# The last quarter of a feed-forward block: the norm carried by the rows, residual additions made by transfers, the last product in the banks of the one before it

## The chip, the cores and the metric

The kernel runs on one core of one Trainium2 chip. The metric is the device time of one execution in microseconds (us). A profile comes from one execution; its span runs from the first to the last instruction and is a little shorter than the time.

## What is computed

One layer of a streaming encoder over 512 frames (columns here) and 1024 channels, then a final norm. Everything is float32. Three branches (banded attention, a gated recurrence and latent attention) are gated, merged and projected, and the result is added to x. The part that matters here is what follows:

```
h2 = rmsnorm(x, norm_ffn_g)                    # x: 512 frames, 1024 channels
x  = x + square(relu(h2 @ w_ff1)) @ w_ff2      # 4096 hidden channels
return rmsnorm(x, final_norm_g)
```

The kernel keeps channels on the 128 partitions and frames in the free dimension, so x is eight tiles `x2[m]` of 128 channels x 512 frames, and a norm needs a sum over partitions, which TensorE makes with a matrix of ones.

## The kernel before, in words

Matrix products are exact to float32 by three matmuls each (`mm3`): every operand is split into a high and a low part, and high x high, high x low and low x high are summed. So each weight block of 128x1024 is cast on ScalarE (`wh`) and its rest taken on VectorE (`wl`) before TensorE can use it. There are two tiles for raw weights (`wr`) and three each for `wh` and `wl`.

The norm's factor rstd per frame is not applied before w_ff1: it is a positive factor per frame, so square(relu(.)) of the unnormed product is taken, and rs2 (rstd squared) is multiplied in behind w_ff2.

The hidden channels are treated in four quarters (`for q in range(4)`). For each, `first(q)` makes eight 128-channel blocks by w_ff1 (`gemm`, 24 matmuls of 512 frames each, tile `p`), squares them on ScalarE into a tile r (`rf`) and forms, for each of four row groups i, the seven operands that a Strassen-Winograd scheme needs: A11, A12, A22, S3, S1, S2, S4, each 128x256 with a high part (`rh`) and a low part (`rl`). "A" and "S" are sums and differences of the quadrants that two hidden halves and two halves of the frames make. Then seven half-size products with w_ff2 follow, 48 matmuls of 256 frames each:

| product | left operand (weights) | right operand | into banks | is taken into |
|---|---|---|---|---|
| 1 | b11 | A11 | `ba` (sa) | c11 |
| 2 | a sum of blocks | S1 | `bc` (sc) | m22 |
| 3 | b21 | A12 | `bb` (sb) | c11 |
| 4 | a sum | S2 | `ba`, on top | m12 |
| 5 | b22 | S4 | `bc`, on top | m12 |
| 6 | a sum | S3 | `ba`, on top | m22 |
| 7 | a sum | A22 | new `bb` (sb) | c21, with `ba` |

The sums of weight blocks are made by transfers: `chain` loads a block through SP's queue (tiles `cw` and `ew`) and adds further blocks to it by adding transfers that POOL issues. `take` copies a pair of banks to a pair of tiles in `out` (ScalarE), or adds it there (VectorE). The four results c11, m12, c21 and m22 (m12 and m22 with a minus sign) are the four quadrants of the residual: half of the frames (th) x half of the channels (ch).

Their sums over quarters 0 to 2 are multiplied by rs2 and added to x2 inside `first(3)` (`residual`, after each row group i). In quarter 3 (`last`) the tiles start afresh, and each quadrant is finished as soon as it is complete: `resid` multiplies by rs2 on VectorE (L1291) and adds to x2 on VectorE (L1294). `squares` squares each piece of x2 on ScalarE (L1314), adds the squares up (L1317) and scales the piece by the final gain on ScalarE, in place (L1318). The first two squares of each half of the frames go to the two parts of a tile `fin`; the other six to scratch tiles from `fw`, whose body is

```
temps.append(temps.pop(0))
return temps[-1]
```

with three tiles in `temps`. `finish_half(th)` sums the squares over the channels with three matmuls of ones (`pst`, L1325), makes 1/sqrt with `rstd_of` (L257, L242 to L251: three scratch tiles v, l and r0, all from `fw`; r0 is the result, rf), multiplies the eight pieces of that half by it (L1331, six on VectorE, two on POOL) and sends them out through SP's queue (L1332).

TensorE's instructions run in the order in which the code issues them (`manual_schedule`). In the other queues a planner sets the order, by the order of the code and by when it thinks that operands are ready; what stands in `urgent()` (weight loads, casts and the adding transfers of `chain`) goes first. Waits between engines are set by what an instruction reads and writes: a tile that is handed out again is not written before its last reader is done. In quarter 3 the code has `finish_half(0)` between products 6 and 7, and `finish_half(1)` at the end.

Of the kernel before, what the change touches and what calls it, by code (L numbers as in the profile page):

```python
# [9 lines left out]
F32 = mybir.dt.float32  # L10
F32R = mybir.dt.float32r
I32 = mybir.dt.int32
AF = mybir.ActivationFunctionType
# [4 lines left out]
S = 512  # L18
P = 128
# [121 lines left out]
def _body(ctx, tc, ap, dbgo):  # L141
# [112 lines left out]
    def rstd_of(new, psum, n, w=S, behind=None):  # L254

        v = new("st_v")[:, :w]
        V.tensor_scalar(v, psum, 1.0 / n, EPS, ALU.mult, ALU.add)  # L257
        return rsqrt(new, v, behind=behind)
# [897 lines left out]
    with ExitStack() as f_ctx:  # L1156
# [4 lines left out]
        def fw(n):  # L1161
            temps.append(temps.pop(0))
            return temps[-1]
# [34 lines left out]
        def pair(x):  # L1198
            return x.rearrange("p (a c) -> p a c", a=2)

        def first(q):

            ops = []
            for i in range(4):
                rh = fp.tile([P, 7, H], F32R, tag="rh", name="rh", bufs=4)
                rl = fp.tile([P, 7, H], F32R, tag="rl", name="rl", bufs=4)
                r = fp.tile([P, 8, H], F32, tag="rf", name="rf", bufs=1)
                a21 = r[:, 7]
                for j in range(2):
# [10 lines left out]
                A.copy(rh[:, 0:3], r[:, 0:3])  # L1220
# [3 lines left out]
                V.tensor_tensor(rl[:, 0:3], r[:, 0:3], f(rh[:, 0:3]), ALU.subtract)  # L1224
                A.copy(rh[:, 3:7], r[:, 3:7])
                V.tensor_tensor(rl[:, 3:7], r[:, 3:7], f(rh[:, 3:7]), ALU.subtract)
                ops.append((rh, rl))
                if q == 3:
                    residual(i)
            return ops  # L1230
# [38 lines left out]
                    start and i == 0 and t % 2 == 0, i == 3, skip_group_check=True)  # L1269


        where = dict(c11=(0, 0, ALU.add), m12=(0, 1, ALU.subtract), c21=(1, 0, ALU.add), m22=(1, 1, ALU.subtract))
        out = {}

        def take(name, banks):

            if name in out:
                for b in range(2):
                    V.tensor_tensor(out[name][b], out[name][b], banks[b], ALU.add)
            else:  # L1280
                out[name] = [act.tile([P, S], F32, tag="act", name=name) for _ in range(2)]
                for b in range(2):
                    A.copy(out[name][b], banks[b])

        def resid(name, b, src, ts=(0, 1)):

            th, ch, op = where[name]
            n = slice(th * H, th * H + H)
            u = out[name][b]
            k = slice(ts[0], ts[-1] + 1)  # L1290
            V.tensor_tensor(pair(u)[:, k], pair(src)[:, k], rs2[:, n].unsqueeze(1).to_broadcast([P, len(ts), H]), ALU.mult)  # L1291
            for t in ts:
                m = ch * 4 + 2 * b + t
                V.tensor_tensor(x2[m][:, n], x2[m][:, n], pair(u)[:, t], op)  # L1294

        def residual(i):

            name = ('c11', 'm12', 'c21', 'm22')[i]
            for b in range(2):
                resid(name, b, out[name][b])  # L1300

        sqs = {}

        def squares(name, b, ts=(0, 1)):
            th, ch, _ = where[name]
            n = slice(th * H, th * H + H)
            for t in ts:
                m = ch * 4 + 2 * b + t
                sq = sqs.setdefault(th, [])
                if len(sq) < 2:  # L1310
                    d = fin[th][:, len(sq)]
                else:
                    d = fw("sq")[:, :H]
                A.activation(d, x2[m][:, n], AF.Square)  # L1314
                sq.append(d)
                if 2 < len(sq) < NK:
                    V.tensor_tensor(sq[len(sq) % 2], sq[len(sq) % 2], d, ALU.add)  # L1317
                A.activation(x2[m][:, n], x2[m][:, n], AF.Copy, scale=g_fin[:, m:m + 1])  # L1318

        def finish_half(th):  # L1320
            n = slice(th * H, th * H + H)
            pst = ptp("pst")[:, :H]
            sq = sqs[th]
            for i, d in enumerate((sq[0], sq[1], sq[-1])):
                T.matmul(pst, ones, d, start=i == 0, stop=i == 2)  # L1325
            rf = rstd_of(fw, pst, D, w=H)
            for i in range(NK // 2):
                o = fp.tile([P, 2, H], F32, tag="xg", name="o", bufs=16)
                for j in range(2):
                    m = 2 * i + j  # L1330
                    (G if m in (2, 5) else V).tensor_tensor(o[:, j], x2[m][:, n], rf, ALU.mult)  # L1331
                nc.sync.dma_start(ap['out'][2 * i * P:2 * (i + 1) * P, n].rearrange("(a p) c -> p a c", p=P), o)  # L1332

        for q in range(4):
            last = q == 3
            (b11, b12), (b21, b22) = ([ap['w_ff2'][q, i, j] for j in range(2)] for i in range(2))
            ts = chain(b11, [b12, b22, b21], "cw", 1)
            t3 = chain(b22, [b12], "ew", 1)
            ops = first(q)
            if last:  # L1340
                out.clear()
                fin = [pair(fp.tile([P, S], F32, tag="xg", name="fin", bufs=16)) for _ in range(2)]
                left = [fp.tile([P, S], F32, tag="xg", name="left", bufs=16) for _ in range(2)]

            def plain(b):
                return [stream(b[i], eng=V) for i in range(2)]

            ba = [psc("sa") for _ in range(2)]
# [4 lines left out]
            take('m22', bc)  # L1353
# [7 lines left out]
            product(ba, ts(), ops, S2, False)  # L1361
            take('m12', ba)
            product(bc, plain(b22), ops, S4, False)
            take('m12', bc)
# [18 lines left out]
            if last:  # L1383
                for b in range(2):
                    for t in range(2):
                        resid('c21', b, bb[b], (t,))
                        squares('c21', b, (t,))
            else:
                take('c21', bb)
        finish_half(1)  # L1390

# [14 lines left out]
```

## Time and profile before

| | |
|---|---|
| median of 3 runs | 954.14 us (952.27 to 956.85) |
| the profiled execution | 951.3 us, span 949.5 us |
| granted TensorE clock, mean | 0.984 |
| busy: PE, DVE, ACT, POOL | 907.1, 657.1, 557.5, 201.4 us |
| quarter 3: `first(3)`, seven products, the rest | from 844.3, 887.9 and 930.4 us of the span |

PE is TensorE's matmuls, PEld its weight loads, DVE VectorE, ACT ScalarE, POOL GpSimd, SP the engine that issues most transfers. A row of the order of instructions gives start and duration in us, engine, line, operation, output <- inputs by the program's names, shapes, a count, and in brackets how long the engine had been idle before and who released it. A row of a group gives busy time and mean ns. A row on transfers gives their count, KB each, and the median us from issue to landing.

### The profile page before, as it was taken

To read this page: it belongs to the slowest core of one execution; us is meant where nothing else is said; L and a number is where in the kernel's file an instruction comes from. 1 tells how busy PE (TensorE), PEld (TensorE's weight loads), DVE (VectorE), ACT (ScalarE), POOL (GpSimd) and SP (SyncE) were. 2 spreads that over 40 slices of the span, in tenths; PEclk is the share of its full clock that TensorE was granted. 3 is DMA by queue.
4 is the path that set the end of the run, shared out by engine and by line. 5 is a ranking of instruction groups with operands and counts; after the bars stand their busy time and mean duration, and the time that the engine had idled before them with its cause. 6 is when DMAs were issued, how large, how long until landed. Compare 5 with 4: busy or idle time off the path is not lost.

```text
span 949.5 us, 13636 instructions
## 1 busy us (share of the span) xinstructions
PE 907.1 (96%) x5070; PEld 784.4 (83%) x5070; DVE 657.1 (69%) x1212; ACT 557.5 (59%) x983; POOL 201.4 (21%) x264
## 2 busy tenths in 40 slices
PE   8889999998998899999999999999999999999993
PEld 6578898987877788888888888889989988998992
DVE  6488888787878869788472454455456745885686
ACT  7556778787776656757552444555365346435663
POOL 4422101111154424333122122001101100110002
PEclk9899999999999999999999999999999999999996
DMA  6865445666666475758689784238835862893522
GB/s 200 212 132 120 91 93 115 140 123 125 139 128 144 97 157 111 155 115 195 137 203 207 165 236 140 89 92 196 227 108 133 209 190 89 182 240 111 132 47 89
DMA packets 42947, 138.08 MB, mean 145 GB/s; under 512 B 5056, under 2 KB 9296, under 8 KB 42880
## 3 DMA queue, kind: packets, MB, share of 16 engines
q0 software_dynamic: 23104, 83.95, 43.8%
q1 hardware_dynamic: 19776, 53.26, 16.8%
q8 instruction: 40, 0.66, 0.3%
q14 instruction: 27, 0.22, 0.1%
HBM read 135.03 MB, written 2.16 MB: 144 GB/s over the span
## 4 chain that ended last, share of the span: by engine, by line
PE 72%; DVE 15%; issue 4%; DMA 4%; ACT 3%; POOL 1%; SPq 0%; DVEq 0%; POOLq 0%; ACTq 0%
PE p L227 6%; PE p L228 6%; PE p L226 6%; PE pj L325 3%; PE pj L321 3%; PE pj L323 3%; PE pg L321 3%; PE pg L325 3%; PE pg L323 3%; PE sa L228 2%; PE sa L227 2%; PE sa L226 2%; PE sc L522 2%; DMA bias<-in_rel 2%; PE po L227 2%
## 5 line engine op out<-in xcount | busy, mean ns | idle before, releaser
L221 ACT CAST wh<-wr 128x1024 fp32r<-128x1024 f32 x64 | 67.2, 1050 | 111.0 <-PE p L227 24.8
L222 DVE TENSOR_TENSOR wl<-wr,wh 128x1024 fp32r<-128x1024 f32 x64 | 78.3, 1223 | 75.9 <-ACT wh L221 67.5
L226 PE MATMUL p<-x2h,wh 128*128 128x512 f32 x256 | 100.0, 391 | 0.0
L227 PE MATMUL p<-x2l,wh 128*128 128x512 f32 x256 | 99.6, 389 | 0.0
L228 PE MATMUL p<-x2h,wl 128*128 128x512 f32 x256 | 99.6, 389 | 0.0
L279 ACT ACTIVATE wl<-wh 128x1024 fp32r<-128x1024 f32 x64 | 67.7, 1057 | 48.4 <-PE pg L325 26.9
L321 PE MATMUL pg<-xgh,wh 128*128 128x512 f32 x192 | 76.7, 400 | 0.0
L325 PE MATMUL pg<-xgh,wl 128*128 128x512 f32 x192 | 76.6, 399 | 0.0
L323 PE MATMUL pg<-xgl,wh 128*128 128x512 f32 x192 | 76.3, 398 | 0.0
L321 PE MATMUL pj<-xgh,wh 128*128 128x512 f32 x160 | 65.0, 406 | 2.4 <-ACT c L429 2.4
L323 PE MATMUL pj<-xgl,wh 128*128 128x512 f32 x160 | 65.7, 410 | 0.0
L325 PE MATMUL pj<-xgh,wl 128*128 128x512 f32 x160 | 64.3, 402 | 0.8 <-DMA wl<-in_w_aqk 0.8
L1256 POOL DMA_DIRECT2D cw<-in_w_ff x16 | 13.7, 858 | 219.2 <-DVE wl L1236 216.4
L226 PEld LDWEIGHTS p<-x2h,wh 128*128 128x128 f32 x256 | 48.1, 188 | 10.1 <-issue 0.2
L227 PEld LDWEIGHTS p<-x2l,wh 128*128 128x128 f32 x256 | 48.1, 188 | 10.1 <-issue 0.2
L228 PEld LDWEIGHTS p<-x2h,wl 128*128 128x128 f32 x256 | 48.1, 188 | 10.0
L227 PE MATMUL sa<-rl,wh 128*128 128x256 f32 x192 | 54.3, 283 | 0.0
L228 PE MATMUL sa<-rh,wl 128*128 128x256 f32 x192 | 54.3, 283 | 0.0
L226 PE MATMUL sa<-rh,wh 128*128 128x256 f32 x192 | 54.3, 283 | 0.0
L1236 DVE TENSOR_TENSOR wl<-cw,wh 128x1024 fp32r<-128x1024 f32 x24 | 29.3, 1223 | 29.9 <-ACT wh L1235 29.9
L1235 ACT CAST wh<-cw 128x1024 fp32r<-128x1024 f32 x24 | 25.2, 1050 | 35.0 <-PE sc L227 11.1
L321 PEld LDWEIGHTS pg<-xgh,wh 128*128 128x128 f32 x192 | 36.9, 192 | 7.8 <-DVE tg L884 0.4
(406 smaller groups left out, 2807.7 us busy)
## 6 DMA issues: line engine op xcount, KB each, us to landing
wr<-in_w_ff SPq DMA_DIRECT2D x56, 512.0 KB, 3.5
wh<-in_w_g POOLq DMA_DIRECT2D x24, 512.0 KB, 3.9
wl<-in_w_g POOLq DMA_DIRECT2D x24, 512.0 KB, 6.1
cw<-in_w_ff POOLq DMA_DIRECT2D x24, 512.0 KB, 5.6
wh<-in_w_br POOLq DMA_DIRECT2D x12, 512.0 KB, 3.8
wl<-in_w_br POOLq DMA_DIRECT2D x12, 512.0 KB, 6.1
wh<-in_w_aqk POOLq DMA_DIRECT2D x8, 512.0 KB, 4.4
wl<-in_w_aqk POOLq DMA_DIRECT2D x8, 512.0 KB, 6.4
```

Source lines behind the costliest of these rows:

```text
L221: A.copy(hi[:, :n], r[:, :n])
L222: (eng or G).tensor_tensor(lo[:, :n], r[:, :n], f(hi[:, :n]), ALU.subtract)
L226: T.matmul(out, wh, xh, start=start, stop=False, **kw)
L227: T.matmul(out, wh, xl, start=False, stop=False, **kw)
L228: T.matmul(out, wl, xh, start=False, stop=stop, **kw)
L279: A.activation(lo, f(hi), AF.Copy, scale=-1.0)
L321: T.matmul(out, wh, xh, start=start, stop=False, **kw)
L323: T.matmul(out, wh, xl, start=False, stop=False, **kw)
L325: T.matmul(out, wl, xh, start=False, stop=stop, **kw)
L522: T.matmul(sc[:, :n], l[:, t * P:(t + 1) * P], r[:, :n], start=i == 0, stop=i == len(scores) - 1)
L1235: A.copy(hi, r)
L1236: V.tensor_tensor(lo, r, f(hi), ALU.subtract)
```

## The change

Only quarter 3 and the code that finishes the residual change.

- The rows carry the norm: in `first(3)` the four quadrants of r are multiplied by rs2 on VectorE, two instructions of 128x512 for each row group, before they are cast and split. So what the seven products of quarter 3 give needs no rs2 any more. The sums of quarters 0 to 2 still get it, with their sign, in place (`residual`).
- Outputs go to the residual by adding transfers: `settle` issues four for each quadrant on POOL, each adding 128x256 inside SBUF to a piece of x2: sixteen in `first(3)`, and twelve behind c11, m12 and m22 of quarter 3. `take` gives m12 and m22 their minus sign. c21 alone is still added by VectorE, piece by piece, straight from the banks.
- The last product is in its forerunner's banks: A22 adds into `ba`, behind S3, where it had two banks of its own. The two `left` tiles go.
- The sum of squares is behind it: `finish_half(0)`, with its `pst` matmuls, stands after the A22 product in the code, and the squares of m22 and c21 after that. The gain's product goes to new tiles (`scaled`) and not in place, and an output product takes two pieces (128x512) in one instruction, the first pair on POOL, the three others on VectorE. Half 1 sends its pieces in the order 2, 3, 0, 1.

```diff
@@ first(q), behind the squares of both j @@
+                if q == 3:
+
+                    for x in (r[:, 0:8:7], r[:, A12:A22 + 1]):
+                        V.tensor_tensor(x, x, pair(rs2), ALU.mult)
                 A.copy(rh[:, 0:3], r[:, 0:3])
@@
-        def take(name, banks):
+        def take(name, banks, sign=1.0):
             if name in out:
                 for b in range(2):
-                    V.tensor_tensor(out[name][b], out[name][b], banks[b], ALU.add)
+                    V.tensor_tensor(out[name][b], out[name][b], banks[b], ALU.add if sign > 0 else ALU.subtract)
             else:
                 out[name] = [act.tile([P, S], F32, tag="act", name=name) for _ in range(2)]
                 for b in range(2):
-                    A.copy(out[name][b], banks[b])
-        def resid(name, b, src, ts=(0, 1)):
...
+                    A.activation(out[name][b], banks[b], AF.Copy, scale=sign)
+        def part(name, b, t):
+            th, ch, _ = where[name]
+            return x2[ch * 4 + 2 * b + t][:, th * H:th * H + H]
+        def settle(name):
+            for b in range(2):
+                for t in range(2):
+                    G.dma_start(part(name, b, t), pair(out[name][b])[:, t], accum_op=ALU.add)
         def residual(i):
...
+            for b in range(2):
+                u = pair(out[name][b])
+                V.scalar_tensor_tensor(u, u, sign, rs2[:, n].unsqueeze(1).to_broadcast([P, 2, H]), ALU.mult, ALU.mult)
+            settle(name)
         def squares(name, b, ts=(0, 1)):
...
+                d = fin[th][:, len(sq)] if len(sq) < 2 else fw("sq")[:, :H]
+                A.activation(d, x, AF.Square)
                 sq.append(d)
                 if 2 < len(sq) < NK:
                     V.tensor_tensor(sq[len(sq) % 2], sq[len(sq) % 2], d, ALU.add)
-                A.activation(x2[m][:, n], x2[m][:, n], AF.Copy, scale=g_fin[:, m:m + 1])
+                A.activation(scaled[th][-1][:, t], x, AF.Copy, scale=g_fin[:, m:m + 1])
-        def finish_half(th):
+        def finish_half(th, order):
...
-                for j in range(2):
-                    m = 2 * i + j
-                    (G if m in (2, 5) else V).tensor_tensor(o[:, j], x2[m][:, n], rf, ALU.mult)
+                (G if i == 0 else V).tensor_tensor(o, o, rf.unsqueeze(1).to_broadcast([P, 2, H]), ALU.mult)
@@ the products of a quarter @@
             take('c11', bb)
             if last:
+                settle('c11')
+            product(ba, ts(), ops, S2, False)
+            take('m12', ba, neg)
+            product(bc, plain(b22), ops, S4, False)
+            take('m12', bc, neg)
+            if last:
+                settle('m12')
                 for b in range(2):
-                    resid('c11', b, out['c11'][b])
                     squares('c11', b)
...
+            product(ba, t3(), ops, S3, False)
+            take('m22', ba, neg)
             if last:
+                settle('m22')
                 for b in range(2):
-                    resid('m12', b, out['m12'][b])
                     squares('m12', b)
-            product(ba, t3(), ops, S3, False)
-            take('m22', ba)
-            if last:
-                finish_half(0)
+                product(ba, ts(), ops, A22, False, tiles_first=True)
+                finish_half(0, (0, 1, 2, 3))
                 for b in range(2):
-                    resid('m22', b, out['m22'][b])
                     squares('m22', b)
-                out['c21'] = left
                 for b in range(2):
-                    resid('c21', b, ba[b])
+                    for t in range(2):
+                        x = part('c21', b, t)
+                        V.tensor_tensor(x, x, pair(ba[b])[:, t], ALU.add)
+                        squares('c21', b, (t,))
             else:
                 take('c21', ba)
-            bb = [pup("sb"), acc("sb")]
-            product(bb, ts(), ops, A22, True, tiles_first=last)
...
-        finish_half(1)
+        finish_half(1, (2, 3, 0, 1))
```

More of the change, by code (lines that the diff above doesn't have):

```diff
@@ L1269, in product @@
                     start and i == 0 and t % 2 == 0, i == 3, skip_group_check=True)
-        where = dict(c11=(0, 0, ALU.add), m12=(0, 1, ALU.subtract), c21=(1, 0, ALU.add), m22=(1, 1, ALU.subtract))
+        where = dict(c11=(0, 0, 1.0), m12=(0, 1, -1.0), c21=(1, 0, 1.0), m22=(1, 1, -1.0))
         out = {}
-        def take(name, banks):
+        def take(name, banks, sign=1.0):
             if name in out:
                 for b in range(2):
-                    V.tensor_tensor(out[name][b], out[name][b], banks[b], ALU.add)
+                    V.tensor_tensor(out[name][b], out[name][b], banks[b], ALU.add if sign > 0 else ALU.subtract)
             else:
@@ new lines, in settle, with residual @@
+        def settle(name):
+            for b in range(2):
+                for t in range(2):
+                    G.dma_start(part(name, b, t), pair(out[name][b])[:, t], accum_op=ALU.add)
+        def residual(i):
+            name = ('c11', 'm12', 'c21', 'm22')[i]
+            th, _, sign = where[name]
+            n = slice(th * H, th * H + H)
+            for b in range(2):
+                u = pair(out[name][b])
+                V.scalar_tensor_tensor(u, u, sign, rs2[:, n].unsqueeze(1).to_broadcast([P, 2, H]), ALU.mult, ALU.mult)
+            settle(name)
@@ L1292, in resid, with squares @@
+        sqs, scaled = [[], []], [[], []]
+        def squares(name, b, ts=(0, 1)):
+            th, ch, _ = where[name]
+            if ts[0] == 0:
+                scaled[th].append(fp.tile([P, 2, H], F32, tag="xg", name="o", bufs=16))
             for t in ts:
                 m = ch * 4 + 2 * b + t
[L1294 to L1314, printed above, removed]
+                x = part(name, b, t)
+                sq = sqs[th]
@@ L1342, in _body @@
                 fin = [pair(fp.tile([P, S], F32, tag="xg", name="fin", bufs=16)) for _ in range(2)]
-                left = [fp.tile([P, S], F32, tag="xg", name="left", bufs=16) for _ in range(2)]
             def plain(b):
                 return [stream(b[i], eng=V) for i in range(2)]
+            neg = -1.0 if last else 1.0
             ba = [psc("sa") for _ in range(2)]
@@ L1352, in _body @@
             product(bc, ts(), ops, S1, True)
-            take('m22', bc)
+            take('m22', bc, neg)
             bb = [pup("sb"), acc("sb")]
```

21 lines of the change are left out of this document (4 added, 17 removed).

## The prediction

> **What bounds the kernel now.** I read the page's busy shares first, then a table of busy time by stage, then the chain of work that ended last, then each engine's own order of instructions in the last 120 us.
>
> ```profile
> PE 907.1 (96%) x5070; PEld 784.4 (83%) x5070; DVE 657.1 (69%) x1212; ACT 557.5 (59%) x983; POOL 201.4 (21%) x264
> ...
> 880.00:887.90 7.90, 7.90 (x37) 6.54 (x36) 3.91 (x5) 3.34 (x6) 0.00 (x0) 1.00 0.40 132
> 916.60:922.40 5.80, 5.80 (x50) 5.76 (x49) 5.73 (x11) 3.83 (x7) 0.00 (x0) 1.00 0.00 0
> 924.70:930.40 5.70, 5.70 (x48) 5.51 (x46) 5.69 (x16) 3.58 (x10) 2.55 (x1) 1.00 0.15 50
> 930.40:936.70 6.30, 0.01 (x1) 0.02 (x1) 6.30 (x18) 2.94 (x9) 2.48 (x2) 0.75 0.38 126
> ```
>
> The rows of stages give the stretch, its length, then busy time and instructions of PE, PEld, DVE, ACT and POOL, the granted clock, the share of the transfer engines and GB/s. Up to 922.4 TensorE is full in every stretch: all that the change frees on other engines there is worth nothing, and any wait that it adds to TensorE is paid in full. The place to gain is the end. From 924.7 to 936.7 VectorE is full, 6.3 us of that with TensorE idle. The rows of that end:
>
> ```profile
> 922.29 0.28 PE L228 MATMUL sa<-rh,wl 128*128 128x256 f32 x1
> 922.96 1.28 PE L1325 MATMUL pst<-fin,ones 128*128 128x256 f32 x4 [0.39 <-DVE fin L1317]
> 924.32 0.47 PE L226 MATMUL sb<-rh,wh 128*128 128x256 f32 x1
> 930.14 0.28 PE L228 MATMUL sb<-rh,wl 128*128 128x256 f32 x1
> 936.71 2.04 PE L1325 MATMUL pst<-fin,ones 128*128 128x256 f32 x4 [6.30 <-DVE fin L1317]
> ...
> 922.06 0.75 DVE L1317 TENSOR_TENSOR fin<-fin,t 128x256 f32<-128x256 f32 x2
> 923.40 1.28 DVE L1279 TENSOR_TENSOR m<-m,sa 128x512 f32<-128x512 f32 x2
> 924.71 0.42 DVE L257 TENSOR_SCALAR t<-pst 128x256 f32<-128x256 f32 x1
> 925.05 1.28 DVE L1291 TENSOR_TENSOR m<-m,rs 128x512 f32<-128x512 f32 x2
> 927.93 2.10 DVE L1331 TENSOR_TENSOR o<-xres,t 128x256 f32<-128x256 f32 x6
> 932.22 0.68 DVE L1291 TENSOR_TENSOR left<-sa,rs 128x512 f32<-128x512 f32 x1
> 933.15 1.08 DVE L1294 TENSOR_TENSOR xres<-xres,left 128x256 f32<-128x256 f32 x3
> 934.15 0.74 DVE L1291 TENSOR_TENSOR left<-sb,rs 128x256 f32<-128x256 f32 x2
> 939.65 0.42 DVE L257 TENSOR_SCALAR t<-pst 128x256 f32<-128x256 f32 x1 [2.41 <-PE pst L1325]
> 942.37 3.16 DVE L1331 TENSOR_TENSOR o<-xres,t 128x256 f32<-128x256 f32 x6
> ...
> 927.85 5.03 POOL L1331 TENSOR_TENSOR o<-xres,t 128x256 f32<-128x256 f32 x2 [22.06 <-DVE t L251]
> 942.51 1.73 POOL L1331 TENSOR_TENSOR o<-xres,t 128x256 f32<-128x256 f32 x2 [9.62 <-DVE t L251]
> 942.71 0.94 DVE L1331 TENSOR_TENSOR o<-xres,t 128x256 f32<-128x256 f32 x1
> ```
>
> Today half 0's sum (first pst) stands between S3 and the A22 product; its outputs hide beside A22. After A22 (930.42) everything waits for VectorE's backlog; the second pst starts at 936.71, its scaling at 939.65, and 9.85 us later the span of 949.5 ends. The execution took 951.3, 1.8 more than its span; the median of the runs shown, 954.14, lies 2.8 above it. I add differences to the median.
>
> **The change at the end.** Between 924.7 and 936.7 VectorE loses the products with rs (two of m at 0.64 each, two of 128x512 and four of 128x256 of left at 0.68 and 0.37: 4.1 us) and twelve additions to xres at 0.36 (4.3 us), and gets four such additions straight from the banks (1.4): 7 us less. So the wait of 6.30 goes. What is late next?
>
> A22 follows S3 at once: its first matmul can go at 922.41 instead of 924.32, 2.1 us with the slow first record, so it would end at 928.3. But it adds into the banks that "take m22" still reads. That read (0.64 for each bank) can start on the first bank before the product ends, as m12's does at 916.13 below; it costs 0.2 us if VectorE is free. Today sums of squares of m12 (L1317, 922.06) stand ahead of it on VectorE. Those now wait for adding transfers and would hold it to about 924.5 if they keep their place, and TensorE behind it: 2.5 us. I take 0.7, nearer to the free case, since no pst asks for the sums at that point any more.
>
> An adding transfer inside SBUF of 128 KB isn't in the trace. Bounds:
>
> ```profile
> wh<-in_w_g POOLq DMA_DIRECT2D x24, 512.0 KB, 3.9
> wl<-in_w_g POOLq DMA_DIRECT2D x24, 512.0 KB, 6.1
> cw<-in_w_ff POOLq DMA_DIRECT2D x24, 512.0 KB, 5.6
> out<-o SPq DMA_DIRECT2D x8, 256.0 KB, 2.2
> ...
> 904.93 0.85 POOL L1256 DMA_DIRECT2D cw<-in_w_ff  x1 [1.98 <-DVE wl L1236]
> 916.13 1.41 DVE L1279 TENSOR_TENSOR m<-m,sc 128x512 f32<-128x512 f32 x2
> ```
>
> From 2.2 (a plain transfer out of SBUF) to 5.6 (adding, four times the size). Adding costs 6.1 - 3.9 = 2.2 for 512 KB, a quarter of it here: 2.2 + 0.55 = 2.75, nearest to the out row in size and place. m12 is taken by 917.54; four issues of 0.86 on POOL follow, the last at about 920.2, landing at 923. [...]
>
> Now the step that I think decides. The scratch tiles come from fw, which hands out three tiles in turn. finish_half(0) takes all three: v, l and rf. It is now written before the squares of m22 and c21. These need six scratch tiles, behind the two fin ones: the third and fourth square of m22 fall on v and l, the first of c21 on rf, the last of c21 on rf again. So the first square of c21 cannot be written before every output product of half 0 has read rf, POOL's too. Before, the order was the same, but half 0 was over by 932.88 (POOL's pair took 5.03 from 927.85), and c21's first sum was not there before 934: it cost nothing. Now half 0 is scaled after A22, and the reuse puts the two halves in series:
>
> - A22 ends (E): 928.3 + 0.7 + 1.2 of early stalls (below) = 930.2.
> - Half 0's pst: 922.96 to 924.71, 1.75. Its scaling: 939.65 to 942.37 in the other half, 2.72. Outputs start at 934.7.
> - Its outputs: three 128x512 products on VectorE, 1.9 at 0.64 each (the two L1291 at 925.05), one on POOL of 2 x 0.87 = 1.73, both started by the same result. The last rows of that fence show that they hinder each other: VectorE's second product took 0.94 beside POOL (0.35 each in the six at 927.93), and POOL's pair took 5.03 behind those six against 1.73 later. Ends: 1.9 (no hindrance) and 1.9 + 0.7 + 1.73 = 4.3 (POOL last of all). I take 3.2: rf is free at 937.9. [...]
> - c21: four squares at 0.45 spacing, sums behind them, pst from 1.4 after rf is free to 4.3 after (2.94 as now, 936.71 to 939.65, since TensorE has idled 7 us again): scaling starts at 942.2.
> - Then 9.85 as now; the output products have the same elements. Span 951.9 to 952.1, say 951.9: +2.4.
>
> **The change before the end.** The rows:
>
> ```profile
> 887.83 1.05 ACT L1235 CAST wh<-cw 128x1024 fp32r<-128x1024 f32 x1 [2.58 <-PE p L227]
> 890.07 0.83 ACT L1220 CAST rh<-rf 128x768 fp32r<-128x768 f32 x1
> 890.81 1.05 ACT L1235 CAST wh<-cw 128x1024 fp32r<-128x1024 f32 x1
> 891.14 0.95 DVE L1224 TENSOR_TENSOR rl<-rf,rh 128x768 fp32r<-128x768 f32 x1
> 892.29 0.28 PE L227 MATMUL sa<-rl,wh 128*128 128x256 f32 x1
> ...
> 847.74 1.05 ACT L221 CAST wh<-wr 128x1024 fp32r<-128x1024 f32 x1 [5.17 <-DMA wr<-in_w_ff]
> 848.82 1.23 DVE L222 TENSOR_TENSOR wl<-wr,wh 128x1024 fp32r<-128x1024 f32 x1 [3.02 <-ACT wh L221]
> 850.23 0.39 PE L228 MATMUL p<-x2h,wl 128*128 128x512 f32 x1
> 846.00:848.00 2.00, 2.00 (x11) 1.65 (x10) 0.00 (x0) 0.26 (x1) 0.85 (x1) 1.00 0.90 274
> ...
> cw<-in_w_ff SPq DMA_DIRECT2D x1, 512.0 KB, 8.1
> wr<-in_w_ff SPq DMA_DIRECT2D x1, 512.0 KB, 6.4
> ```
>
> Costed at nothing: the sign in the takes (same instructions, same sizes). The squares of c11 wait for transfers issued from 905.8 (behind the last cw transfer, POOL 904.93 + 0.85), landing from 908.5; they take the place of additions that VectorE made there too. ACT's casts for the next products stand behind them, and three wh tiles let a cast be one half product late; past that cover each us that a square waits is one on TensorE. residual(i): sixteen additions (0.42) go, eight products (0.69) stay, eight row products of 0.69 come: 12.2 to 11.0 on VectorE. POOL gets 28 transfers of 0.86, 24 us; the two cw transfers of this quarter may stand behind eight of them (7 us), and their data is first used at 887.83. SP's order is unchanged.
>
> Two places have no slack. The second row product (0.69) stands between the square, over just before 890.07, and the cast to rh. rl was done at 892.09 for a matmul at 892.29; now 892.8, a stall of 0.5, or 1.4 if the cw cast (1.05) slips ahead of the rh cast. I take 0.8. At 847.7 a weight load landed just in time (wl done 850.05, used 850.23) with the transfer engines 90% busy; residual's sixteen transfers fall there. Between 0 and 1.7 (that load took 6.4, a cw load beside it 8.1); I take 0.4. Together 1.2.
>
> **The rivals.** *Faster: the scratch tiles don't bind.* If c21's squares could run as their sums come, both pst stand back to back behind A22: 930.2 + 1.75 + 1.75 + 2.72 + 1.0 (half 0's outputs on VectorE in between) + 3.16 + 3.97 = 944.6, 4.9 less: 949.2. For it: VectorE's 7 us are really gone. Against: the turn of three is in the code. *Slower by over 0.5%: late adding transfers hold A22.* If they land after 5.6 like cw's, VectorE reaches "take m22" 2.9 us later, with the products waiting: 959.4. It passes +0.5% (4.8 us) from a landing of some 5.2. For it: the order of L1317 and L1279 on VectorE today, and 917 to 923 is short for four transfers. Against: nothing else is moved there (DMA share 0.00 from 916.6). *The change does nothing at the end*: the gain at A22 and the wait removed equal the new wait; that is the forecast without its early stalls, 955.3.
>
> **How the numbers follow.** Forecast 954.14 + 2.4 = 956.5. 0.5% is about what a measurement of this kernel can tell from no change; with the third rival the forecast has 64 in 100. Its own ends: E from 929.0 (stalls 0.2 and 0.5) to 932.7 (2.5 more, two thirds of what all upper bounds together add), rf free 1.3 earlier or 1.1 later: span 949.4 to 955.5, time 954 to 960. Free scratch tiles 10, late transfers 18, other stalls from a changed order of casts 8. Range 951.5 to 962: it leaves out the faster rival and the last tail. Faster 0.10, same 0.64, slower 0.26.
>
> **What would show it.** Right: A22's first matmul within 1 us of S3's last, pst directly behind A22, then some 7 us of idle TensorE; ACT squares of c21 waiting for output products; gaps of TensorE near 850 and 892. Wrong: c21 squares running before half 0's outputs, or a gap of more than 2.5 us before A22.

## The result: slower by about 1%, and the profile after

The changed kernel takes 963.92 us (median of 5 runs, 961.29 to 966.59), the kernel before 955.98 (5 runs, 952.27 to 956.85). The ratio on record is 1.0098, 95% interval 1.0078 to 1.0118, which is 9.4 us on 955.98 (the two medians alone lie 7.9 apart). The forecast was 2.4 us slower, and 962.0 was the top of its range.

The profiled execution of after took 966.59 us, with a span of 964.8. It is the slowest of the five, at the lowest mean clock (0.974; the others 0.977 to 0.984). Its last quarter began 6.4 us later than before's. Of these 6.3 were there when the feed-forward block began, ahead of all the code that the change touches. The rows of the block's first line of matmuls by w_ff1 (count, shortest, median and longest ns, from first to last up to 700 us) and the first such matmul of quarter 3, two rows of before and then two of after:

```profile
L226 PE MATMUL p<-x2h,wh x99: 389/389/798, 591.9 to 699.7; 128*128 128x512 f32 x99
```

```profile
844.31 0.40 PE L226 MATMUL p<-x2h,wh 128*128 128x512 f32 x1
```

```profile
L226 PE MATMUL p<-x2h,wh x89: 389/389/798, 598.2 to 699.3; 128*128 128x512 f32 x89
```

```profile
850.70 0.40 PE L226 MATMUL p<-x2h,wh 128*128 128x512 f32 x1
```

So this lag is not the change's. From here on each kernel is measured by "quarter 3": from its first matmul by w_ff1 to the end of the span.

Before it is 949.5 - 844.31 = 105.2 us. After: 964.8 - 850.70 = 114.1, so 8.9 more, about the 9.4 of the ratio. The page of after has these busy times; VectorE lost 10 us and POOL gained 20, as the change says, and yet the kernel got slower:

```profile
PE 914.7 (95%) x5070; PEld 790.2 (82%) x5070; DVE 646.6 (67%) x1170; ACT 557.3 (58%) x983; POOL 221.6 (23%) x290
```

The table of busy time by stage of after, from the end of S3 (columns as in the prediction: stretch, length, PE, PEld, DVE, ACT, POOL, clock, share of the transfer engines, GB/s):

```profile
929.86:933.92 4.06, 0.00 (x0) 0.03 (x1) 2.39 (x4) 3.31 (x8) 1.09 (x2) 0.74 0.69 99
933.92:941.84 7.92, 7.92 (x48) 7.92 (x49) 1.88 (x5) 3.92 (x10) 3.49 (x4) 0.70 0.48 69
941.84:943.34 1.50, 1.46 (x8) 0.95 (x6) 0.76 (x3) 0.84 (x2) 0.00 (x0) 1.00 0.00 0
943.34:950.86 7.52, 0.00 (x0) 0.03 (x1) 5.82 (x11) 3.70 (x10) 1.39 (x1) 0.64 0.31 102
953.80:964.80 11.00, 0.00 (x0) 0.00 (x0) 4.24 (x6) 1.25 (x3) 1.68 (x1) 0.50 0.29 95
```

Where before had 0.39 for a pst and then A22 at full clock, after has 4.06 us of idle TensorE, and then an A22 that takes 7.92 us up to the pst, at a mean clock of 0.70. The pst comes directly behind it, and then TensorE idles for 7.52 us, both as forecast. The finer table shows when the clock changed: a mean of 0.91 from 931 to 932 puts its fall to 0.50 at 931.8, and 0.67 from 938 to 939 puts its return to 1.00 at 938.7.

```profile
931.00:932.00 1.00, 0.00 (x0) 0.00 (x0) 0.09 (x2) 1.00 (x2) 0.00 (x0) 0.91 0.92 131
932.00:938.00 6.00, 4.08 (x19) 4.11 (x20) 3.05 (x5) 2.46 (x7) 3.49 (x4) 0.50 0.57 82
938.00:939.00 1.00, 1.00 (x8) 1.00 (x8) 0.00 (x0) 1.00 (x4) 0.00 (x0) 0.67 0.94 135
939.00:941.84 2.84, 2.84 (x26) 2.84 (x25) 0.75 (x2) 1.94 (x5) 0.00 (x0) 1.00 0.08 11
```

The order of the engines in after (start, duration, engine, line, operation; idle time and its releaser in brackets) shows what the 4.06 us wait for:

```profile
912.65 3.72 POOL L1297 DMA_DIRECT2D xres<-c  x4
919.52 0.42 ACT L1321 ACTIVATE fin<-xres 128x256 f32<-128x256 f32 x1 [3.33 <-DMA xres<-c]
921.74 1.03 ACT L1239 CAST wh<-ew 128x1024 fp32r<-128x1024 f32 x1
924.27 1.04 ACT L1239 CAST wh<-ew 128x1024 fp32r<-128x1024 f32 x1
...
925.34 1.22 DVE L1240 TENSOR_TENSOR wl<-ew,wh 128x1024 fp32r<-128x1024 f32 x1 [0.91 <-ACT wh L1239]
926.48 1.28 DVE L1283 TENSOR_TENSOR m<-m,sc 128x512 f32<-128x512 f32 x2
927.46 3.49 POOL L1297 DMA_DIRECT2D xres<-m  x4 [11.08 <-DVE m L1283]
930.17 0.42 ACT L1321 ACTIVATE t<-xres 128x256 f32<-128x256 f32 x1 [3.91 <-DMA xres<-m]
930.89 1.03 ACT L1239 CAST wh<-cw 128x1024 fp32r<-128x1024 f32 x1
931.95 1.23 DVE L1240 TENSOR_TENSOR wl<-cw,wh 128x1024 fp32r<-128x1024 f32 x1 [0.91 <-ACT wh L1239]
933.10 1.28 DVE L1283 TENSOR_TENSOR m<-m,sa 128x512 f32<-128x512 f32 x2
933.92 0.55 PE L226 MATMUL sa<-rh,wh 128*128 128x256 f32 x1 [4.06 <-DVE m L1283]
```

Read it from the top. The four transfers for c11 are issued from 912.65; ScalarE stands 3.33 us for the first of them. Behind that square, in ScalarE's order, are the two casts of ew, S3's weights. VectorE takes their rests before "take m12", so that take comes at 926.48, and m12's transfers go out from 927.46. ScalarE then stands 3.91 us for those, with the last cast of A22's weights (cw) behind the square. Only at 930.89 can it cast; VectorE takes the rest and behind it m22, and A22 starts. Two waits on transfers, one behind the other, through the casts that share ScalarE's queue. The transfers of after (count, KB each, median us from issue to landing): cw, then the three groups of four adding ones inside SBUF, for c11, m12 and m22 (the last two rows, in this order). Behind them the share of the transfer engines (next to last column) while c11's were on their way:

```profile
cw<-in_w_ff POOLq DMA_DIRECT2D x2, 512.0 KB, 5.5
xres<-c POOLq DMA_DIRECT2D x4, 128.0 KB, 6.6
xres<-m POOLq DMA_DIRECT2D x4, 128.0 KB, 3.3
xres<-m POOLq DMA_DIRECT2D x4, 128.0 KB, 3.7
```

```profile
914.00:920.00 6.00, 6.00 (x53) 6.00 (x52) 1.80 (x2) 1.53 (x3) 2.37 (x3) 1.00 1.00 169
```

**Where the 8.9 us are.** The prediction showed before's rows; against these, after has:

| step | before | after | more |
|---|---|---|---|
| A11's rl, product 1 | no gap | gap 0.42, product 0.7 longer | 0.7 |
| end of S3 to first matmul of A22 | 922.57 to 924.32 | 929.86 to 933.92 | 2.3 |
| other small gaps up to A22 | | | 0.2 |
| A22, to the end of its last matmul | 6.1 | 8.1 | 2.0 |
| A22's end to the scaling of half 1 | 930.42 to 939.65 | 942.00 to 953.80 | 2.6 |
| that scaling to the end of the span | 9.85 | 11.0 | 1.15 |

### The profile page after: what moved, and what is told of

Read it like the earlier page. It is cut to its first block, busy times and chain, and to the rows that moved or that the text cites. A ratio compares the mean times of both kernels' runs of the same rounds, so it can differ in the third digit from the quotient of the medians.

```text
span 964.8 us, 13639 instructions
## 1 busy us (share of the span) xinstructions
PE 914.7 (95%) x5070; PEld 790.2 (82%) x5070; DVE 646.6 (67%) x1170; ACT 557.3 (58%) x983; POOL 221.6 (23%) x290
## 4 chain that ended last, share of the span: by engine, by line
PE 56%; DVE 15%; issue 12%; DMA 7%; ACT 6%; POOL 3%; DVEq 0%; POOLq 0%; ACTq 0%
PE p L228 5%; PE p L227 5%; PE p L226 5%; PE pj L325 2%; PE pj L321 2%; PE pj L323 2%; PE pg L325 2%; PE pg L323 2%; PE pg L321 2%; PE sa L226 2%; PE sa L227 2%; PE sa L228 2%; PE sc L522 2%; PE po L227 2%; PE po L228 2%
## 5 line engine op out<-in xcount | busy, mean ns | idle before, releaser
L226 PE MATMUL sa<-rh,wh 128*128 128x256 f32 x208 | 59.9, 288 | 4.1 <-DVE m L1283 4.1
L227 PE MATMUL sa<-rl,wh 128*128 128x256 f32 x208 | 59.9, 288 | 0.4 <-DVE rl L1228 0.4
L228 PE MATMUL sa<-rh,wl 128*128 128x256 f32 x208 | 59.9, 288 | 0.0
L226 PEld LDWEIGHTS sa<-rh,wh 128*128 128x128 f32 x208 | 41.0, 197 | 4.4 <-ACT o L1325 4.2
```

Source lines behind the costliest of these rows:

```text
L226: T.matmul(out, wh, xh, start=start, stop=False, **kw)
L227: T.matmul(out, wh, xl, start=False, stop=False, **kw)
L228: T.matmul(out, wl, xh, start=False, stop=stop, **kw)
```

## The experiments

All start from the changed kernel unless said otherwise. Each ratio is to runs of the kernel before, taken for the experiments. "Gap" is the idle time of TensorE ahead of A22.

**e1_own_scratch.** The six squares of half 1 that went to scratch tiles get tiles of their own.

```diff
-                d = fin[th][:, len(sq)] if len(sq) < 2 else fw("sq")[:, :H]
+                if len(sq) < 2:
+                    d = fin[th][:, len(sq)]
+                elif th == 0:
+                    d = fw("sq")[:, :H]
+                else:
+                    d = own[len(sq) // 2 - 1][:, len(sq) % 2]
```

> The changed kernel, but the six squares of half 1 that took turns on the three scratch tiles get tiles of their own. Measure: quarter 3, from the first gemm of first(3) to the end of the span (before 105.2 us, changed 114.1), and A22's end to the scaling of half 1 (before 9.2, changed 11.8). Theory 'the reuse of the scratch tiles puts the halves in series': the second pst no longer waits for half 0's output products; 11.8 falls to 4 to 5.5 (two pst of 1.75 and what squares ScalarE is late with), quarter 3 to about 107.5; A22's wait of 4.1 stays. Rival 'the sums are late because m22's adding transfers and ScalarE's backlog are': 11.8 falls by no more than 2, quarter 3 stays above 112.

Ratio to before 1.0036 (1.0018 to 1.0054), quarter 3 110.2: 3.9 less than after. The gap stays 4.06. The rows of this kernel:

```profile
936.41 1.08 PE L1337 MATMUL pst<-fin,ones 128*128 128x256 f32 x4
939.45 2.96 DVE L1340 TENSOR_TENSOR o<-o,t 128x512 f32<-128x512 f32 x3
942.33 0.41 DVE L257 TENSOR_SCALAR t<-pst 128x256 f32<-128x256 f32 x1
```

The second pst now runs directly behind the first, so the reuse of scratch tiles did put the halves in series, as forecast. But from A22's end to the scaling of half 1 it is still 7.05 us, where 4 to 5.5 were expected: the scaling (L257) stands behind half 0's three output products on VectorE. One wait gone, the next one is the order of VectorE.

**e2_casts_first.** Squares and gains of half 0 are placed behind the last cast of weights on ScalarE.

```diff
+                after(A.activation(d, x, AF.Square), last_cast[0])
...
                 settle('m22')
-                for b in range(2):
-                    squares('m12', b)
                 product(ba, ts(), ops, A22, False, tiles_first=True)
+                for name in ('c11', 'm12'):
+                    for b in range(2):
+                        squares(name, b)
```

> The changed kernel, but on ScalarE the squares and gains of half 0 stand behind the last cast of weights, so no cast waits for an adding transfer. Theory 'ScalarE's queue: squares that wait for transfers hold the casts, these hold take m12, the next transfers and the weights of A22': A22's wait falls from 4.1 to under 1, A22 runs at full clock (6.1 and not 8.1), quarter 3 falls from 114.1 to 108.5 to 109.5. Rival 'the shared banks: A22 must wait for take m22 in any case': the wait stays above 2.5, quarter 3 above 112.

**e3_vector_adds.** In the last quarter c11, m12 and m22 are added to x2 by VectorE, not by transfers; the order stays.

```diff
-                    G.dma_start(part(name, b, t), pair(out[name][b])[:, t], accum_op=ALU.add)
+                    x, y = part(name, b, t), pair(out[name][b])[:, t]
+                    if last:
+                        V.tensor_tensor(x, x, y, ALU.add)
+                    else:
+                        G.dma_start(x, y, accum_op=ALU.add)
```

> The changed kernel, but c11, m12 and m22 of quarter 3 are added to x2 by VectorE (twelve 128x256 additions) and not by transfers; the sixteen transfers in first(3) stay. Theory 'the landing of the transfers is the root': no square waits for a transfer, A22's wait falls to under 1 with its full clock, quarter 3 to 108.5 to 109.5, as with the casts first; 4.3 us more on VectorE before A22 cost nothing. Rival 'VectorE had no room': its additions stand in front of take m22 and A22 still waits 2 us or more; quarter 3 above 111.

e2: ratio 1.0024 (1.0006 to 1.0043), quarter 3 107.95. e3: 1.0024 (1.0005 to 1.0044), 107.4. Six to seven us less than after, each. The first matmul of A22, in e2 and then in e3, and the A22 stage of e2:

```profile
924.85 0.35 PE L226 MATMUL sa<-rh,wh 128*128 128x256 f32 x1 [0.16 <-DVE m L1285]
```

```profile
923.83 0.35 PE L226 MATMUL sa<-rh,wh 128*128 128x256 f32 x1 [0.26 <-DVE m L1283]
```

```profile
924.85:930.70 5.85, 5.85 (x49) 5.85 (x50) 3.14 (x8) 5.42 (x16) 3.49 (x4) 1.00 0.65 94
```

Either taking the squares off the casts' way or taking the transfers away closes the gap, and in e2 A22 then ran at full clock (1.00): 6.0 us to the end of its last matmul, against 8.1 in after and 6.1 in before. So neither the transfers alone nor the shared banks cost the time: the banks cost 0.16. It is the pair of a late landing and casts that stand behind the square that waits for it (ScalarE's 3.33 and 3.91 us in after).

**e4_both.** e1 and e2 together.

> The changed kernel with both edits: own scratch tiles, and half 0's squares behind the last cast. Theory: both costs go, and they add, since one lies ahead of A22's end and one behind it: quarter 3 at 102 to 103.5 against 105.2 before, 0.2 to 0.3% faster than before. Rival 'they overlap': the squares of half 0 that now come later hold the first pst, or ScalarE has sixteen squares and gains left behind A22; quarter 3 stays at 105 or more.

Ratio 0.9992 (0.9971 to 1.0013), quarter 3 103.9, a little over the forecast. The sum is done, and its scaling comes late:

```profile
933.17 0.70 PE L1339 MATMUL pst<-own,ones 128*128 128x256 f32 x2 [0.16 <-ACT own L1328]
933.77 2.96 DVE L1342 TENSOR_TENSOR o<-o,t 128x512 f32<-128x512 f32 x3
936.65 0.41 DVE L257 TENSOR_SCALAR t<-pst 128x256 f32<-128x256 f32 x1
```

The pst is over at 933.87; its scaling waits until 936.65 for half 0's products, as in e1. With both waits off, the change is no better than before within the interval.

**e12_m12_held** and **e13_c11_held** take e2 apart: only m12's squares, or only c11's, go behind the last cast; in the code they are moved behind the A22 product. e12 has the lines below; in e13 the name is 'c11'.

```diff
+        def hold(i, name):
+            if name == 'm12':
+                after(i, last_cast[0])
```

> The changed kernel, but of half 0's squares only m12's stand behind the last cast of weights; c11's stay ahead of the ew casts. Changed kernel: ScalarE waited 3.3 us for c11's transfers (landed after 6.8) and 3.9 us for m12's (2.7), the second wait with the cast of A22's weights behind it. Theory 'the second wait holds A22, the first only makes it later': A22's wait falls from 4.1 to under 0.7, quarter 3 from 114.1 to 108 to 109. Rival 'the first wait alone is enough': take m12, the ew rest and take m22 stay late, A22 waits 2 us or more, quarter 3 above 111.

> The reverse: only c11's squares stand behind the last but one cast; m12's stay where they were, one of them ahead of the cast of A22's last weights. Theory: with no wait for c11 take m12 comes 3 us earlier, its transfers land near the end of S3, and the cast behind the one square of m12 is late by 1 us at most: A22 waits under 1.5, quarter 3 at 108 to 110. Rival 'm12's landing holds A22 by itself': A22 waits 2.5 us or more and runs at the low clock, quarter 3 above 112.

e12: ratio 1.0049 (1.0025 to 1.0072), quarter 3 110.9. e13: 1.0029 (1.0005 to 1.0053), 108.8. e13 came out as expected; e12 lies between its two theories, whose bounds were a gap under 0.7 or of 2 and more. ScalarE waited 2.90 for c11 in e12 and 2.04 for m12 in e13. The rows of e12:

```profile
924.38 0.42 DVE L1330 TENSOR_TENSOR fin<-fin,t 128x256 f32<-128x256 f32 x1 [0.60 <-ACT t L1327]
924.73 1.28 DVE L1285 TENSOR_TENSOR m<-m,sa 128x512 f32<-128x512 f32 x2
925.55 0.36 PE L226 MATMUL sa<-rh,wh 128*128 128x256 f32 x1 [1.75 <-DVE m L1285]
```

its table by stretch behind that start (clock in the third column from the end):

```profile
926.20:927.00 0.80, 0.80 (x7) 0.80 (x6) 0.56 (x2) 0.63 (x3) 0.80 (x3) 0.62 0.30 50
927.00:928.00 1.00, 1.00 (x6) 1.00 (x6) 0.00 (x0) 0.71 (x2) 1.00 (x3) 0.50 0.93 135
929.00:930.00 1.00, 1.00 (x7) 1.00 (x6) 0.00 (x0) 0.84 (x3) 0.19 (x1) 0.60 0.92 134
930.00:931.00 1.00, 1.00 (x11) 1.00 (x10) 0.75 (x2) 1.00 (x3) 0.00 (x0) 1.00 0.92 131
```

and the first matmul of A22 in e13:

```profile
923.43 0.36 PE L226 MATMUL sa<-rh,wh 128*128 128x256 f32 x1 [1.00 <-DVE m L1285]
```

So each of the two squares alone leaves a smaller gap, 1.75 or 1.00, and together they make 4.06: the first wait makes the second one's transfers late. In e12 "take m22" does stand behind a sum of squares that waits for a transfer, the very thing that the prediction's slower rival named; in after it stood behind the last rest of weights instead. And e12's gap of only 1.75 us was followed by a half clock for 3.4 us, e13's gap of 1.00 was not.

**e9_rows_alone.** The kernel before, with the norm carried by the rows and nothing else of the change.

```diff
+                if q == 3:
+                    for x in (r[:, 0:8:7], r[:, A12:A22 + 1]):
+                        V.tensor_tensor(x, x, pair(rs2), ALU.mult)
...
-            V.tensor_tensor(pair(u)[:, k], pair(src)[:, k], rs2[:, n].unsqueeze(1).to_broadcast([P, len(ts), H]), ALU.mult)
+            if normed:
+                u = src
+            else:
+                V.tensor_tensor(pair(u)[:, k], pair(src)[:, k], rs2[:, n].unsqueeze(1).to_broadcast([P, len(ts), H]), ALU.mult)
...
+                normed.append(True)
```

> The kernel before with one part of the change alone: the rows carry the norm, so that quarter 3's residual additions need no products with rs2. Theory: product A11 waits 0.4 to 0.7 us at its last row group, as in the changed kernel; VectorE has 4.1 us less to do behind S3, and the wait of 6.3 us behind A22 falls by about 4: quarter 3 from 105.2 to 101.5 to 103. Rival 'ScalarE's squares take VectorE's place as the last': the wait falls by under 2 and quarter 3 stays at 104 or more.

Ratio 0.9977 (0.9952 to 1.0002), quarter 3 102.25, 3 us under before. The wait of the second pst, 6.30 before, is about half:

```profile
933.64 2.17 PE L1333 MATMUL pst<-fin,ones 128*128 128x256 f32 x4 [3.31 <-DVE fin L1325]
```

The product rows cost what was forecast (a gap of 0.42 at A11) and give back 3 us of VectorE's backlog. The part by itself is a small gain; by the interval it is not quite told from none.

**e6_pool_last.** e4, with the output that POOL makes sent last in the code.

```diff
+            for i in (1, 2, 3, 0):
+                k, o = order[i], scaled[th][i]
                 nc.sync.dma_start(ap['out'][2 * k * P:2 * (k + 1) * P, n].rearrange("(a p) c -> p a c", p=P), o)
```

> The run with both edits (own scratch tiles, half 0's squares behind the last cast), and in each half the output that POOL makes is sent last through SP's queue, not first. Measure: scaling of the half 1 to the end of the span (before 9.85 us, changed 11.0, with both edits 11.15). Theory 'in SP's queue the three outputs of VectorE stand behind POOL's': the first output goes 1 us earlier, 11.15 falls to 10.0 to 10.4, quarter 3 from 103.9 to about 103. Rival 'four transfers of 256 KB are bound by their bytes': the last one still lands when it did, 11.15 falls by under 0.3.

Ratio 0.9995 (0.9973 to 1.0016), quarter 3 104.2: no effect, since the planner put POOL's transfer first all the same; the first transfer left at the end of POOL's product, 1.88 us after rf. The question went to e11.

**e7_norm_first.** e6, with half 1's sum and scaling written ahead of half 0's outputs, in tiles of its own.

```diff
-                finish_half(0, (0, 1, 2, 3))
+                rf0 = norm_half(0)
...
+        rf1 = norm_half(1)
+        finish_half(0, (0, 1, 2, 3), rf0)
+        finish_half(1, (2, 3, 0, 1), rf1)
```

> The same, and half 1's sum and scaling are written ahead of half 0's output products, with scratch tiles of their own. With both edits half 1's scaling was ready to start near 933.1 but stood behind half 0's three output products on VectorE until 936.65. Theory 'VectorE's queue order': A22's end to the scaling of half 1 falls from 7.8 to about 4.5, and 2 to 3 of the 3.3 us show at the end: quarter 3 at 100 to 101.5. Rival 'the output products and their transfers take their time in any case': the end moves by under 1 us.

Ratio 0.9956 (0.9933 to 0.9979), quarter 3 101.9, a little above the forecast. The scaling of half 1 came 0.18 us behind its pst, so VectorE's order was the wait of e1 and e4. About 1 us of it came back at the end: from scaling to end 12.1 against 11.1, as half 0's products now stand in between.

**e8_sum_inside.** e3, with e1's tiles, tiles of their own for half 1's norm, POOL's output last in the code as in e6, and half 0's sum inside A22, behind its first quarter.

```diff
+                product(ba, w7, ops, A22, False, tiles_first=True, tt=(0,))
+                rf0 = norm_half(0)
+                product(ba, w7, ops, A22, False, tiles_first=True, tt=(1, 2, 3))
```

> The changed kernel with VectorE's additions for the last quarter's residual, own scratch tiles, POOL's output sent last, and half 0's sum of squares inside A22, behind its first quarter, not behind the whole product. Theory: half 0 is scaled and sent beside A22 as before the change, TensorE waits for nothing but the last squares of c21: quarter 3 at 98.5 to 101, faster than before by 0.4 to 0.7%. Rival 'half 0's products on VectorE hold c21's additions': 102 or more.

Ratio 0.9957 (0.9933 to 0.9981), quarter 3 101.5, short of the forecast: half 0's products stood ahead of c21's last two additions on VectorE, and the second pst waited 3.21 us for them.

**e10_outputs_later.** e8, with half 0's outputs written behind c21's additions.

```diff
-                finish_half(0, (0, 1, 2, 3), rf0)
...
+        finish_half(0, (0, 1, 2, 3), rf0)
         rf1 = norm_half(1)
```

> The run with half 0's sum inside A22, and half 0's output products are written behind c21's additions. There the second pst waited 3.2 us for the sums of squares: VectorE had half 0's three output products (2.96 us) ahead of c21's last two additions. Theory 'VectorE's queue order': that wait falls by 1 to 2 us, quarter 3 from 101.5 to 99.5 to 100.5. Rival 'the products only change places, with the three outputs now behind half 1's scaling': quarter 3 stays within 0.5 of 101.5.

Ratio 0.9934 (0.9909 to 0.9960), median 947.26, quarter 3 100.7: faster than both kernels and the lowest ratio of all, though its interval overlaps those of e7 and e8. The wait of the second pst fell from 3.21 to 2.37, less than forecast: one of half 0's products (1.76 us from 932.32) still stood ahead of c21's last two additions.

```profile
935.74 0.70 PE L1340 MATMUL pst<-fin,ones 128*128 128x256 f32 x2 [2.37 <-DVE fin L1333]
936.90 0.42 DVE L257 TENSOR_SCALAR norm<-pst 128x256 f32<-128x256 f32 x1 [0.62 <-PE pst L1340]
```

**e11_pool_last_forced.** e10, with POOL's output held behind the others on SP's queue.

```diff
+                d = nc.sync.dma_start(...)
+                if i == 0:
+                    after(d, prev)
+                prev = d
```

> The same, and POOL's output is held behind VectorE's three in SP's queue by an order that the planner must keep. In the earlier run that moved it in the code alone, the queue still had POOL's first (its first transfer left at the end of POOL's product, 1.88 us after rf), so that edit had changed nothing. Theory 'VectorE's outputs stand behind POOL's': the first transfer leaves 0.7 to 0.9 us after rf instead of 1.88, and the end comes 0.5 to 1.0 us earlier than without the order. Rival 'bound by the last product': the last transfer leaves when it did, the end moves by under 0.3.

Ratio 0.9962 (0.9941 to 0.9983), quarter 3 101.5. The first transfer left 0.8 us behind rf, the last one at 943.82, and from scaling to end it took 10.10 against 10.30 in e10. So the first transfer's wait for POOL is nearly all hidden; that the last product and the transfers behind it set the end is argued, not shown. Quarter 3 is 0.8 longer than e10's even so, because the clock fell at 935.4, just ahead of the last matmuls of the second pst, which took 2.1 us for e10's 1.1.

## Why the prediction was wrong

**What held.** The scratch tiles: from A22's end to the scaling of half 1 it took 11.8 us, 12.0 were forecast, and e1 shows the mechanism. The terms fit one by one: sum 1.3 (1.75 forecast), scaling 2.9 (2.7), outputs 3.15 (3.2), and from there to the next scaling 4.4 (4.3). ScalarE's last squares of c21 do wait for VectorE's outputs:

```profile
949.50 0.72 ACT L1321 ACTIVATE t<-xres 128x256 f32<-128x256 f32 x2 [2.52 <-DVE o L1335]
```

The backlog of VectorE is gone. A11's stall was 0.7 against 0.8. An adding transfer of 128 KB landed in 2.7 us where nothing was in front of it, 2.75 forecast. SP's and POOL's queues in `first(3)` cost nothing: it took 43.5 us in both kernels. The stall near 850 (0.4 forecast) did not come.

**What failed, in the order of the steps.** The prediction's own sign of being wrong came, a gap of more than 2.5 us ahead of A22.

1. "Costed at nothing: ... The squares of c11 wait for transfers ... landing from 908.5". They landed 6.5 to 6.8 us after issue, behind two adding transfers of 512 KB for cw on the same queue (5.5 us each, share of the transfer engines 1.00 from 914 to 920). The prediction named the cover (casts half a product ahead) and said that each us past it is one on TensorE; it sized the wait by a transfer that runs alone. Whether the queue's order or the full transfer engines held them, no run separates. e13 against e2 and after prices it: with c11 held back, the gap is 1.00, not 4.06.
2. "I take 0.7" for A22's stall. This is the term that decided: TensorE waited 4.06, so A22 began 2.3 us later behind S3 than before, where it should have begun 1.4 earlier (2.1 less 0.7). The reason given for a small value, that no pst asks for the sums any more, looked at VectorE alone. ScalarE's squares had no such freedom; the last cast of A22's own weights stood behind one. The slower rival (18 in 100) had the right victim, "take m22" and A22 behind a landing, but another delay: m12's transfers, landing after 5.6 us, hold the sums on VectorE, 5.3 us slower in all. They landed in 2.7 to 4.6 us; late by 3 us was their issue, because c11's landing had held the casts. The wait that this rival named, in a sum of squares ahead of "take m22", only e12 shows.
3. The granted clock. The forecast had A22 at full clock; after the gap it ran at half (0.50) for 4.7 us (933.9 to 938.7) and took 2.0 us longer. How long it stayed low under A22 differs between the profiled executions: 4.7 us in after, 5.9 in e1, 3.4 in e12 (last section). The prediction counted a slower pst (2.94 us to its scaling, for 1.75) behind 7 us of idle time, as before's rows show it, but nothing of the kind for a product behind a stall.
4. "Then 9.85 as now". It took 11.0. Of the 1.15 more, 0.45 lies ahead of the last byte and 0.7 behind it. The output products are of the same elements, but the first transfer now leaves at the end of POOL's one product of 128x512, 1.88 us after rf, where it left after 1.35:

```profile
956.73 1.68 POOL L1335 TENSOR_TENSOR o<-o,t 128x512 f32<-128x512 f32 x1 [9.07 <-DVE t L251]
958.43 0.37 SPq L1336 DMA_DIRECT2D out<-o  x1
```

e11 shows that an earlier first transfer gives back only 0.2, so this is not shown to be all of the 0.45. The 0.7 is the time from the last byte to the end of the span: 2.4 us in after, 1.7 in before. It goes with the adding transfers of quarter 3's outputs: it is 2.4 in all eight kernels that have them (after, e1, e2, e4, e6, e7, e12, e13) and 1.7 in all six that don't (before, e3, e8 to e11), and e3 differs from after in nothing else. By what mechanism stays open.

Steps 1 to 3 carry the miss. Of the 6.5 us between the 2.4 forecast and the 8.9 found, A22's late start and its low clock make 5.7 and the tail 1.15; the other terms came out some 0.5 smaller than forecast. Between after and e2 the gap goes from 4.06 to 0.16 and A22 from 8.1 to 6.0, 6.0 us in all, and quarter 3 is 6.15 shorter. What is left of the loss in e2 (107.95 against 105.2, 2.75 us) was forecast for the most part: the halves in series 2.6 and A11 0.7, less the 1.7 that A22 now gains (0.16 us from S3's end to its start for 1.75, and 6.0 for 6.1), and the tail's 1.15, which was not.

Of the rivals, "the scratch tiles don't bind" falls with e1: even with tiles of their own the two scalings would not have come together, since VectorE's order was next.

**Where the gain went.** VectorE's 7 us are real: e9, e7 and e10 each show part of them as time. In the changed kernel they went into a wait of ScalarE for transfers, a low clock, and a reuse of three tiles. e10 keeps what the change is for, rows that carry the norm and a last product in shared banks, and drops the adding transfers of quarter 3's outputs, the shared scratch and the sum behind A22.

## What to carry to other kernels

Before work is handed from an engine to a transfer, look at what stands behind its first reader on that reader's own queue: here a square that waited for a landing held a cast of weights, and a wait of 3.3 us made the next transfers 3 us late. Price a transfer with what is under way ahead of it at that moment (here 6.5 to 6.8 us behind two of 512 KB), not by the row of one that ran alone (2.7 us). When a long wait is taken out of a kernel's end, list the next three in order (tiles handed out in turn, the order of the scaling on VectorE, the last outputs), because each of e1, e4 and e8 gained less than forecast through the next one.

## What the runs showed of the hardware

The granted clock around A22, read from tables in steps of 0.1 us:

| run | gap ahead of A22 | clock at 0.50 | A22 |
|---|---|---|---|
| after | 929.86 to 933.92 | 931.8 to 938.7, again from 945.5 | 8.1 |
| e1 | 922.65 to 926.71 | 925.7 to 932.6, again from 942.8 | 8.6 |
| e12 | 923.80 to 925.55 | 926.4 to 929.8, again from 936.6 | 7.5 |
| e13 | 922.43 to 923.43 | not before 932.9 | 6.0 |

The changes lie 6.9 and 6.8 us apart in after, 6.9 and 10.2 in e1, 3.4 and 6.8 in e12; what sets their times these runs do not show. The price of a gap was not the same in each: behind the same 4.06 us A22 took 8.1 us in after and 8.6 in e1, against 6.1 at full clock in before, and in e12, behind 1.75 us, the clock fell 0.8 us after TensorE had resumed and cost 1.5. A gap of 1.00 us did not lower it under A22 (e13). In after the clock fell 2.0 us after S3's last matmul. How long a gap has to be for the clock to fall was not tried.

Adding transfers of 128 KB inside SBUF took 2.7 us as the first of four and 4.6 as the last (m12's in after), 6.5 to 6.8 behind two of 512 KB, and up to 14.4 in `first(3)`. Three products of 128x512 took 2.96 us on VectorE beside one on POOL, where 1.9 was worked out for them alone.
